# Dense products of a two-block transformer layer: float32 operands once instead of three float32r products of split operands

## The chip, the cores and the metric

The kernel runs on one core of one Trainium2 chip. The metric is device time in microseconds (us) for one execution of the whole program; the time before is the median of three runs. TensorE (PE) does the matrix products, VectorE (DVE), ScalarE (ACT) and GpSimd (POOL) the elementwise work, SyncE (SP) issues most of the transfers.

## The reference

512 tokens of width 1024 pass through two blocks. All arrays are float32.

```python
# first block
u = rms_norm(x, mix_norm_g) @ w_in                    # 1024 -> 2816
c = conformer_conv(u[..., :512])                      # 31 taps over 256 channels
a = dilated_attention(q, k, v, positions)             # 12 heads of 64, over 512 keys
x = x + concat(rms_norm(c), rms_norm(a)) @ w_out
x = x + memory_cross_attention(rms_norm(x), rms_norm(mem), w_xq, w_xk, w_xv, w_xo)   # 256 memory rows, 4 heads of 256
x = x + hierarchical_moe(rms_norm(x), ...)            # 32 experts, 1024 -> 512 -> 1024, 2 per token
x = rms_norm(x, final_norm_g)
# second block
u = rms_norm(x, norm_mix_g_2) @ w_in_2
ya = forgetting_attention(q, k, v, f)                 # 8 heads of 64, causal
ys = s5(u_ssm, ...)                                   # state space layer, then a gate with w_glu_2
x = x + (gate_a * (ya @ w_proj_attn_2) + gate_s * (ys @ w_proj_ssm_2)) @ w_out_2
x = x + hier_moe(rms_norm(x), ...)                    # 32 experts, 1024 -> 256 -> 1024, 2 per token
```

## The kernel before

The program is one long instruction stream; an order of instructions is worked out when it is built, and tc.issue_after fixes single places by hand. It has four stages, one after the other: dense1 (the first block up to its experts), the first expert layer (Moe, method experts), dense2 (the second block up to its experts), the second expert layer.

Dense products. An operand is kept as two float32r tiles, a rounded part (hi) and the rest (lo). Activations lie transposed in a pair of tiles of 128 x 8 x 512, made by K.pair. K.put (L195) fills one 512-column piece of a pair from PSUM: ScalarE writes hi (L199, L202), VectorE then writes lo, the difference (L200, L203). Weights come in units of 1024 x 256, 1 MB, by K.load_unit (L135, issued by SP at L141) into a ring of two slots, k.wt. K.split (L118) makes hi on ScalarE (L125) and lo on VectorE or, every third time, on GpSimd (L128), in two halves for a unit, in a pool of two buffers. Each product is then three matmuls by K.mm3 (L114, L115, L116): hi with hi, hi with lo, lo with hi.

Two helpers loop over the pieces. K.tok_mm (L172) has the activations stationary and 256 weight columns moving: 8 row chunks x 4 token blocks = 32 products for a unit. K.col_mm (L184) has 128 weight columns stationary and up to 512 tokens moving: 8 chunks x 2 = 16 products for a unit. Counted by the code, there are 1024 products with 256 moving columns: 288 in the nine units of q, k and v of dense1, 128 in memory keys and values, 128 in w_out, 32 in the scores of the memory attention, 128 in w_xo, 64 in v of dense2, 128 in its q and k, 128 in w_out_2 (and these sum to 1024). There are 360 with 512 columns: 32 in the convolution's two units, 64 in w_xq, 16 in the memory attention's values, 32 in the two u units of dense2, 64 in its first gate, 8 in the forget logits (L1836, 8 stationary columns), 16 in w_glu_2, 32 in w_proj_ssm_2, 64 in its second gate, 32 in w_proj_attn_2.

Attention. K.heads_T (L151) splits q and k of two heads, transposes them with 12 float32r transposes (L168) and copies them out with 6 copies on ScalarE (L170); it is called 20 times. The scores of a block of 128 queries are two matmuls, q with k hi and q with k lo (L536, L537 in dense1, 48 blocks of 512 keys; L1974, L1975 in dense2, 32 blocks of 128, 256, 384 and 512 keys). The softmaxed block is transposed by four float32 transposes (L545) and multiplied with v in plain float32 (L552): four products of 64 columns for a block.

Experts. Their products take plain float32 operands already. Two experts share the array, 64 stationary columns each: 8 chunks x 512 columns up (L1086), then down (L1108). The second layer works on one further unit, extra_up, in which one expert has all 128 stationary columns: 8 such products. Weights stream in through slots; the first 18 loads of the first layer and 17 of the second are issued during the dense stage before it. The last expert pairs' outputs go back by a one-hot product in float32r, hi and lo (scatter, L1123, L1124), added to X by VectorE (L1126).

The start of dense2 (L1754 to L1836): X is transposed (L1766) and put into the pair hT; the first unit of w_in_2 is loaded after the last ScalarE step of the expert layer before it (tc.issue_after(k.last.ins), L1824) and split; norms() gives Rb (L1790), by which VectorE scales the unit's results; then come the forget logits and the second u unit.

Of the kernel before, what the change touches and what calls it, by code (L numbers as in the profile page):

```python
# [10 lines left out]
F32 = mybir.dt.float32  # L11
F32R = mybir.dt.float32r
# [3 lines left out]
AF = mybir.ActivationFunctionType  # L16
# [11 lines left out]


def f(ap):  # L30
    return ap.bitcast(F32)
# [27 lines left out]
class K:  # L59
# [9 lines left out]
    def setup(self):  # L69
# [9 lines left out]
        self.identr = c.tile([128, 128], F32R, name="identr")  # L79
        nc.vector.tensor_copy(self.identr, self.ident)  # L80
# [16 lines left out]
    def pair(self, pool):  # L97
        return tuple(pool.tile([128, KC, S], F32R, name="b") for _ in range(2))

# [10 lines left out]
    def mm3(self, out, st, mv, start, stop):  # L110
        nc = self.nc
        sh, sl = st
        mh, ml = mv
        nc.tensor.matmul(out, sh, mh, start=start, stop=False, skip_group_check=True)  # L114
        nc.tensor.matmul(out, sh, ml, start=False, stop=False, skip_group_check=True)  # L115
        nc.tensor.matmul(out, sl, mh, start=False, stop=stop, skip_group_check=True)  # L116

    def split(self, pool, pieces, eng=None):  # L118

        nc = self.nc  # L120
        out = []
        for src, kc, n in pieces:
            hi = pool.tile([128, 4, 256], F32R, name="wh")
            lo = pool.tile([128, 4, 256], F32R, name="wl")
            nc.scalar.activation(hi[:, :kc, :n], src, AF.Copy)  # L125
            self.n += 1
            e = eng or (nc.gpsimd if self.n % 3 == self.pool_mod else nc.vector)
            e.tensor_sub(lo[:, :kc, :n], src, f(hi[:, :kc, :n]))  # L128
            for c in range(kc):
                out.append((hi[:, c, :n], lo[:, c, :n]))  # L130
        return out

    pool_mod = 0

    def load_unit(self, cols, kc=8):  # L135

        t = self.wt().rearrange("p (c n) -> p c n", c=8)
        o = 0
        for c in cols:
            w = c.shape[1]  # L140
            self.nc.sync.dma_start(t[:, :kc, o:o + w], c.rearrange("(c p) n -> p c n", p=128))  # L141
            o += w
        return t[:, :kc, :o]

    def split_unit(self, spool, t, eng=None):
        return self.split(spool, [(t[:, j:j + 4], 4, t.shape[2]) for j in range(0, t.shape[1], 4)], eng)

    def unit(self, spool, cols, kc=8):
        return self.split_unit(spool, self.load_unit(cols, kc))

    def heads_T(self, wk, tpt, r4, qT, kh, kl, i):  # L151


        nc = self.nc
        V = nc.vector
        Rq = wk.tile([128, 2, 2, 2, 64], F32R, name="Rq", bufs=1)
        Rk = wk.tile([128, 2, 2, 2, 2, 64], F32R, name="Rk", bufs=1)
        nc.scalar.activation(Rq[:, :, :, 0], r4[:, :, 0:2], AF.Copy)
        V.tensor_sub(Rq[:, :, :, 1], r4[:, :, 0:2], f(Rq[:, :, :, 0]))
        for t in range(2):  # L160
            nc.scalar.activation(Rk[:, :, :, 0, t], r4[:, :, 2:4], AF.Copy)
            V.tensor_sub(Rk[:, :, :, 1, t], r4[:, :, 2:4], f(Rk[:, :, :, 0, t]))
        for dst, mk in ((qT, lambda b, h: Rq[:, b, h]), (kh, lambda b, h: Rk[:, b, h, 0]), (kl, lambda b, h: Rk[:, b, h, 1])):
            p = tpt()
            for h in range(2):
                for b in range(2):
                    o = (2 * h + b) * 128
                    nc.tensor.transpose(p[:, o:o + 128].bitcast(F32R), mk(b, h).rearrange("p t i -> p (t i)"), self.identr)  # L168
            for h in range(2):
                nc.scalar.activation(dst[h][:, 256 * i:256 * i + 256], p[:, 256 * h:256 * h + 256], AF.Copy)  # L170

    def tok_mm(self, act, ws, tiles, nb, n, first=True, last=True, kcs=None):  # L172
# [3 lines left out]
        for i, c in enumerate(ks):  # L176
            for b in range(nb):
# [43 lines left out]
    def raw_T(self, psum, xb, gcol, hi, lo, nb, tag="tp", tpb=2):  # L221

        nc = self.nc
        for c in range(KC):
# [4 lines left out]
            self.put((hi, lo), np.s_[:, c, :w], ps[:, :w], gcol[:, c:c + 1])  # L229
# [9 lines left out]
    def norm_T(self, work, psum, xb, gcol, hi, lo, nb, tpb=2):  # L239
# [11 lines left out]
        for c in range(KC):  # L251
# [4 lines left out]
            nc.scalar.activation(hi[:, c, :w], ps[:, :w], AF.Copy, scale=gcol[:, c:c + 1])  # L256
            nc.vector.scalar_tensor_tensor(lo[:, c, :w], ps[:, :w], gcol[:, c:c + 1], f(hi[:, c, :w]),
# [1899 lines left out]
```

## Time and profile before

| | us |
|---|---|
| median of the runs (1734.44, 1736.08, 1739.26) | 1736.08 |
| the profiled execution | 1743.17 |
| its span, first to last instruction | 1741.5 |
| PE, busy in the span | 1575.2 |
| VectorE, busy | 769.0 |
| ScalarE, busy | 542.6 |
| GpSimd, busy | 381.8 |

The profiled execution is 7.1 us longer than the median of the runs, and 1.7 us of it lie outside the span. PE's matmuls are pipelined: the listed time of one is longer than the distance from its start to the next one's, so busy time tells that PE had work, not how fast it went through it. The distance of starts in the timeline is the cost of one in a row of them. One line of the source can make more than one matmul record.

### The profile page before, as it was taken

To read this page: it belongs to the slowest core of one execution; us is meant where nothing else is said; L and a number is where in the kernel's file an instruction comes from. 1 tells how busy PE (TensorE), PEld (TensorE's weight loads), DVE (VectorE), ACT (ScalarE), POOL (GpSimd) and SP (SyncE) were. 2 spreads that over 40 slices of the span, in tenths; PEclk is the share of its full clock that TensorE was granted. 3 is DMA by queue.
4 is the path that set the end of the run, shared out by engine and by line. 5 is a ranking of instruction groups with operands and counts; after the bars stand their busy time and mean duration, and the time that the engine had idled before them with its cause. 6 is when DMAs were issued, how large, how long until landed. Compare 5 with 4: busy or idle time off the path is not lost. (4 is left out here: it accounts for less than half of the span.)

```text
span 1741.5 us, 24303 instructions
## 1 busy us (share of the span) xinstructions
PE 1575.2 (90%) x9241; PEld 1073.1 (62%) x9241; DVE 769.0 (44%) x1977; ACT 542.6 (31%) x1207; POOL 381.8 (22%) x525
## 2 busy tenths in 40 slices
PE   7999999999999898888988768999999999898986
PEld 5999999987973333332323346888888894333332
DVE  8985546646374311111101356734664547211224
ACT  5355566535212111010100033242655422111111
POOL 2311111110132641532420031111231411111110
PEclk9999999999989999999999888999999999998997
DMA  6234344124669999999999796527440946999984
GB/s 197 80 112 143 97 133 158 62 97 152 224 193 400 425 425 424 424 424 425 425 424 426 327 152 74 114 74 90 64 71 30 364 158 225 387 417 416 398 342 157
DMA packets 171225, 423.71 MB, mean 243 GB/s; under 512 B 20605, under 2 KB 107828, under 8 KB 143328
## 3 DMA queue, kind: packets, MB, share of 16 engines
q1 hardware_dynamic: 133616, 378.08, 60.0%
q0 software_dynamic: 12080, 24.03, 4.6%
q10 hardware_dynamic: 25408, 20.00, 3.7%
q8 instruction: 74, 1.21, 0.3%
q14 instruction: 47, 0.39, 0.1%
HBM read 403.38 MB, written 35.27 MB: 252 GB/s over the span
## 5 line engine op out<-in xcount | busy, mean ns | idle before, releaser
L1086 PE MATMUL h<-w,xgr 128*64 128x512 f32 (+1 forms) x752 | 220.9, 612 | 22.1 <-DMA w<-in_w_dram 19.7
L1086 PE MATMUL h<-b,xgr 128*64 128x512 f32 x800 | 224.3, 607 | 16.8 <-DMA b<-in_w_dram 15.4
L115 PE MATMUL mm<-wl,b 128*128 128x256 f32 x832 | 236.1, 285 | 3.7 <-POOL wl L128 3.6
L114 PE MATMUL mm<-wh,b 128*128 128x256 f32 x832 | 235.7, 286 | 1.4 <-ACT b L202 0.8
L116 PE MATMUL mm<-wh,b 128*128 128x256 f32 x832 | 234.5, 284 | 0.0
L128 POOL TENSOR_TENSOR wl<-w,wh 128x1024 fp32r<-128x1024 f32 x38 | 99.1, 2610 | 557.2 <-ACT wh L125 487.8
L125 ACT ACTIVATE wh<-w 128x1024 fp32r<-128x1024 f32 x112 | 118.3, 1058 | 171.2 <-PE mm L115 72.0
L115 PEld LDWEIGHTS mm<-wl,b 128*128 128x128 f32 x832 | 158.8, 191 | 5.2 <-POOL wl L128 4.0
L114 PEld LDWEIGHTS mm<-wh,b 128*128 128x128 f32 x832 | 158.2, 191 | 3.4 <-ACT b L202 1.0
L116 PEld LDWEIGHTS mm<-wh,b 128*128 128x128 f32 x832 | 158.3, 191 | 0.6
L1108 PE MATMUL o<-b,hgT 128*64 128x512 f32 x448 | 135.6, 652 | 18.0 <-DVEq L1335 9.3
L1086 PEld LDWEIGHTS h<-b,xgr 128*64 128x64 f32 x800 | 68.8, 138 | 124.9 <-issue 87.9
L1086 PEld LDWEIGHTS h<-w,xgr 128*64 128x64 f32 (+1 forms) x752 | 64.9, 141 | 130.7 <-issue 89.6
L114 PE MATMUL mm<-b,wh 128*128 128x512 f32 x320 | 127.0, 409 | 13.3 <-ACT b L202 11.5
L115 PE MATMUL mm<-b,wh 128*128 128x512 f32 x320 | 129.7, 406 | 1.2 <-DVE b L203 1.2
L116 PE MATMUL mm<-b,wl 128*128 128x512 f32 x320 | 127.2, 401 | 3.0 <-POOL wl L128 2.7
L1090 DVE SCALAR_TENSOR_TENSOR hg<-h,gate,hg 128x512 f32<-128x512 f32 (+1 forms) x32 | 19.7, 617 | 246.9 <-PE h L1086 179.6
L128 DVE TENSOR_TENSOR wl<-w,wh 128x1024 fp32r<-128x1024 f32 x74 | 95.0, 1283 | 53.0 <-ACT wh L125 52.3
L1108 PE MATMUL o<-w,hgT 128*64 128x512 f32 (+1 forms) x328 | 97.7, 629 | 4.4 <-ACT og L1137 2.2
L1108 PEld LDWEIGHTS o<-b,hgT 128*64 128x64 f32 x448 | 41.7, 149 | 85.0 <-issue 72.1
L1089 ACT ACTIVATE hg<-h,gate 128x512 f32<-128x512 f32 (+1 forms) x32 | 18.6, 581 | 215.0 <-PE h L1086 185.3
L114 PEld LDWEIGHTS mm<-b,wh 128*128 128x128 f32 x320 | 61.3, 193 | 28.9 <-ACT b L202 12.2
(673 smaller groups left out, 2769.7 us busy)
## 6 DMA issues: line engine op xcount, KB each, us to landing
b<-in_w_dram SPq DMA_DIRECT2D x106, 1024.0 KB
w<-in_w_dram SPq DMA_DIRECT2D x86, 1024.0 KB
b<-in_w_expert_down_dram SPq DMA_DIRECT2D x20, 1024.0 KB
w<-in_w_expert_gate_dram SPq DMA_DIRECT2D x36, 512.0 KB
w<-in_w_expert_up_dram SPq DMA_DIRECT2D x36, 512.0 KB
w<-in_w_in_dram SPq DMA_DIRECT2D x17, 1024.0 KB
b<-in_w_expert_gate_dram SPq DMA_DIRECT2D x30, 512.0 KB
b<-in_w_expert_up_dram SPq DMA_DIRECT2D x30, 512.0 KB
```

Source lines behind the costliest of these rows:

```text
L114: nc.tensor.matmul(out, sh, mh, start=start, stop=False, skip_group_check=True)
L115: nc.tensor.matmul(out, sh, ml, start=False, stop=False, skip_group_check=True)
L116: nc.tensor.matmul(out, sl, mh, start=False, stop=stop, skip_group_check=True)
L125: nc.scalar.activation(hi[:, :kc, :n], src, AF.Copy)
L128: e.tensor_sub(lo[:, :kc, :n], src, f(hi[:, :kc, :n]))
L1086: nc.tensor.matmul(h[po], xg[:, c, ss], fw[e][c], start=c == 0, stop=c == KC - 1, skip_group_check=True)
L1089: nc.scalar.activation(hg, a, AF.Silu, scale=r)
L1090: nc.vector.scalar_tensor_tensor(hg, b, r, hg, op0=OP.mult, op1=OP.mult)
L1108: nc.tensor.matmul(o[po], hT[:, j, po], W[2][e][half * nt + j], start=j == 0, stop=j == nt - 1, skip_group_check=True)
```

## The change

Every dense product takes its float32 operands as they are, in one matmul call. mm3, the splits of weights and activations, pair and the lo tiles go; put is one instruction, on ScalarE and VectorE in turn; weights lie raw in a ring of four slots. heads_T makes four float32 transposes and two copies, the scores are one call with 64 rows in the contraction. The one-hot products of scatter are one float32 call. The second gate of dense2 (sga) moves from bigR to bigL, and the outputs of its two branches share one tile.

```diff
-    def pair(self, pool):
-        return tuple(pool.tile([128, KC, S], F32R, name="b") for _ in range(2))
+    def big(self, pool):
+        return pool.tile([128, KC, S], F32, name="b")
...
-    def mm3(self, out, st, mv, start, stop):
-        nc = self.nc
-        sh, sl = st
-        mh, ml = mv
-        nc.tensor.matmul(out, sh, mh, start=start, stop=False, skip_group_check=True)
-        nc.tensor.matmul(out, sh, ml, start=False, stop=False, skip_group_check=True)
-        nc.tensor.matmul(out, sl, mh, start=False, stop=stop, skip_group_check=True)
-
-    def split(self, pool, pieces, eng=None):
...
-            nc.scalar.activation(hi[:, :kc, :n], src, AF.Copy)
...
-            e.tensor_sub(lo[:, :kc, :n], src, f(hi[:, :kc, :n]))
...
+    def mm(self, out, st, mv, start, stop):
+        self.nc.tensor.matmul(out, st, mv, start=start, stop=stop, skip_group_check=True)
...
-        for dst, mk in ((qT, lambda b, h: Rq[:, b, h]), (kh, lambda b, h: Rk[:, b, h, 0]), (kl, lambda b, h: Rk[:, b, h, 1])):
-            p = tpt()
-            for h in range(2):
-                for b in range(2):
-                    o = (2 * h + b) * 128
-                    nc.tensor.transpose(p[:, o:o + 128].bitcast(F32R), mk(b, h).rearrange("p t i -> p (t i)"), self.identr)
-            for h in range(2):
-                nc.scalar.activation(dst[h][:, 256 * i:256 * i + 256], p[:, 256 * h:256 * h + 256], AF.Copy)
+        p = tpt()
+        for j in range(2):
+            for b in range(2):
+                o = (2 * j + b) * 128
+                nc.tensor.transpose(p[:, o:o + 128], r4[:, b, 2 * j:2 * j + 2].rearrange("p h i -> p (h i)"), self.ident)
+        nc.scalar.activation(qT[:, 256 * i:256 * i + 256], p[:, 0:256], AF.Copy)
+        nc.vector.tensor_copy(kT[:, 256 * i:256 * i + 256], p[:, 256:512])
...
-                self.mm3(o, (act[0][:, c, bs], act[1][:, c, bs]), (ws[i][0][:, :n], ws[i][1][:, :n]), st, sp)
+                self.mm(o, act[:, c, bs], ws[i][:, :n], st, sp)
...
-                self.mm3(o, (ws[c][0][:, ms], ws[c][1][:, ms]), (act[0][:, act_c0 + c, :width], act[1][:, act_c0 + c, :width]), st, sp)
-
-    def put(self, dst, dsl, ps, scale=None):
+                self.mm(o, ws[c][:, ms], act[:, act_c0 + c, :width], st, sp)
+
+    def put(self, dst, ps, scale=None):
+
         nc = self.nc
-        h, l = dst[0][dsl], dst[1][dsl]
+        self.n += 1
+        if self.n % 2:
+            return nc.scalar.activation(dst, ps, AF.Copy, scale=1.0 if scale is None else scale)
         if scale is None:
-            nc.scalar.activation(h, ps, AF.Copy)
-            return nc.vector.tensor_sub(l, ps, f(h))
-        else:
-            nc.scalar.activation(h, ps, AF.Copy, scale=scale)
-            return nc.vector.scalar_tensor_tensor(l, ps, scale, f(h), op0=OP.mult, op1=OP.subtract)
+            return nc.vector.tensor_copy(dst, ps)
+        return nc.vector.tensor_scalar(dst, ps, scale, None, op0=OP.mult)
...
-        spool = k.pool("splA", 2, st, side="right")
+        k.wt = Slots([k.ring] * 2 + [k.pool("ringA", 2, st, side="right")] * 2)
...
-                    nc.tensor.matmul(p, qT[:, bs], kh, start=True, stop=False)
-                    marks.append(nc.tensor.matmul(p, qT[:, bs], kl, start=False, stop=True).ins)
+                    marks.append(nc.tensor.matmul(p, qT[:, bs], kT, start=True, stop=True).ins)
...
-            oh, ol = og[:, 0], og[:, 1]
-            self.k.last = nc.scalar.activation(oh, outs[half], AF.Copy, scale=gate)
-            nc.vector.scalar_tensor_tensor(ol, outs[half], gate, f(oh), op0=OP.mult, op1=OP.subtract)
+            self.k.last = nc.scalar.activation(og[:, half], outs[half], AF.Copy, scale=gate)
...
-                nc.tensor.matmul(y, sT[:, bs], oh, start=True, stop=False)
-                nc.tensor.matmul(y, sT[:, bs], ol, start=False, stop=True)
+                nc.tensor.matmul(y, sT[:, bs], og[:, half], start=True, stop=True)
...
-        spool = k.pool("splD", 2, st)
+        k.wt = Slots([k.ring] * 2 + [k.pool("ringD", 2, st)] * 2)
...
         with tc.issue_after(k.last.ins):
-            ws = k.split_unit(spool, k.load_unit([w_in[:, 1544:1800]]), G)
+            ws = k.load_unit([w_in[:, 1544:1800]])
...
-        ysT = k.big_r.tile([128, KC, S], F32R, name="b")
-        ysT = (ysT[:, 0:4], ysT[:, 4:8])
+        yT = k.big(k.big_r)
+        ysT, yaT = yT[:, 0:4], yT[:, 4:8]
...
-        sga = k.big_r.tile([128, KC, S], F32, name="b")
-        yaT = k.big_r.tile([128, KC, S], F32R, name="b")
-        yaT = (yaT[:, 0:4], yaT[:, 4:8])
+        sga = k.big(k.big_l)
```

## Rows read from the trace of the kernel before

**Rows 1.** The page: busy share of PE and of the transfers in 40 slices, in tenths.
```profile
PE   7999999999999898888988768999999999898986
...
DMA  6234344124669999999999796527440946999984
```

**Rows 2.** Busy time by stage: dense1, experts, dense2, experts; experts' middle; dense2's start.
```profile
core 0: us, PE busy (x) PEld busy (x) DVE busy (x) ACT busy (x) POOL busy (x), PEclk, DMA share, GB/s
0.00:495.00 495.00, 468.86 (x3518) 440.72 (x3518) 303.27 (x661) 247.08 (x562) 90.05 (x97) 0.98 0.41 134
495.00:1011.40 516.40, 450.14 (x1974) 180.37 (x1974) 138.27 (x463) 64.60 (x141) 154.95 (x267) 0.97 0.97 395
1011.40:1432.00 420.60, 392.51 (x2645) 343.92 (x2643) 226.54 (x504) 179.24 (x372) 93.67 (x86) 0.96 0.54 117
1432.00:1741.50 309.50, 263.72 (x1106) 108.09 (x1106) 100.93 (x353) 51.72 (x132) 43.11 (x76) 0.91 0.85 336
522.00:958.00 436.00, 382.69 (x1665) 144.66 (x1663) 89.08 (x300) 54.58 (x121) 146.83 (x254) 0.98 1.01 422
...
1011.40:1066.00 54.60, 36.07 (x143) 25.02 (x142) 38.46 (x129) 15.25 (x30) 17.47 (x18) 0.75 0.84 145
```

**Rows 3.** Groups of PE's instructions by line and form: the split products' largest.
```profile
L115 PE MATMUL mm<-wl,b 128*128 128x256 f32 x832 | 236.1, 285 | 3.7 <-POOL wl L128 3.6 <-DVE wl L128 0.2
L115 PE MATMUL mm<-b,wh 128*128 128x512 f32 x320 | 129.7, 406 | 1.2 <-DVE b L203 1.2
```

**Rows 4.** Timeline of PE, two stretches of float32r products (start us, us): first and last.
```profile
1198.81 0.28 PE L114 MATMUL mm<-wh,b 128*128 128x256 f32 x1
...
1199.89 0.28 PE L114 MATMUL mm<-wh,b 128*128 128x256 f32 x1
...
1175.73 0.40 PE L116 MATMUL mm<-b,wl 128*128 128x512 f32 x1
...
1178.06 0.40 PE L116 MATMUL mm<-b,wl 128*128 128x512 f32 x1
```

**Rows 5.** Float32 products, PE's groups by form: an expert with the whole array; attention's values.
```profile
L1086 PE MATMUL h<-w,xgr 128*128 128x512 f32 x16 | 8.8, 674 | 0.5 <-ACT xgr L1182 0.5
L552 PE MATMUL po<-v,pT 128*128 128x64 f32 x384 | 48.4, 272 | 0.1
```

**Rows 6.** Timeline of PE: float32 records of 512 and 64 columns in a row.
```profile
1627.85 2.74 PE L1086 MATMUL h<-w,xgr 128*128 128x512 f32 x6
...
308.93 1.00 PE L552 MATMUL po<-v,pT 128*128 128x64 f32 x8
```

**Rows 7.** Timeline of PE: transposes in a row, of float32 (L545) and float32r (L168).
```profile
186.03 1.04 PE L545 MATMUL tp<-ident,ml 128*128 128x128 f32 x8
...
1319.15 0.87 PE L168 MATMUL tp<-identr,Rk 128*128 128x128 f32 x8
```

**Rows 8.** PE's waits, whole span: us in total, times, longest.
```profile
PE mm L114 <- ACT b L202: 12.3, 2, 11.5
...
PE y L1123 <- DVE X L1126: 5.0, 6, 1.7
...
PE mm L115 <- POOL wl L128: 3.8, 3, 2.7
...
PE tp L1790 <- DVE r L1787: 3.4, 1, 3.4
PE mm L116 <- POOL wl L128: 2.7, 1, 2.7
...
PE mm L114 <- ACT wh L125: 2.0, 4, 1.0
```

**Rows 9.** Timeline, start of dense2.
```profile
1011.40 1.03 PE L1766 MATMUL tp<-ident,X 128*128 128x128 f32 x8
...
1020.06 2.00 ACT L125 ACTIVATE wh<-w 128x1024 fp32r<-128x1024 f32 x2 [14.41 <-DMA w<-in_w_in_dram]
...
1023.91 1.22 PE L114 MATMUL mm<-b,wh 128*128 128x512 f32 x2 [11.48 <-ACT b L202]
...
1063.67 0.40 PE L116 MATMUL tp<-b,wfl 128*8 128x512 f32 x1
```

More of the change, by code (lines that the diff above doesn't have):

```diff
@@ L142, in load_unit, with heads_T @@
             o += w
[L143 to L151, printed above, removed]
-        nc = self.nc
[L155 to L162, printed above, removed]
-        for dst, mk in ((qT, lambda b, h: Rq[:, b, h]), (kh, lambda b, h: Rk[:, b, h, 0]), (kl, lambda b, h: Rk[:, b, h, 1])):
-            p = tpt()
-            for h in range(2):
-                for b in range(2):
-                    o = (2 * h + b) * 128
-                    nc.tensor.transpose(p[:, o:o + 128].bitcast(F32R), mk(b, h).rearrange("p t i -> p (t i)"), self.identr)
-            for h in range(2):
-                nc.scalar.activation(dst[h][:, 256 * i:256 * i + 256], p[:, 256 * h:256 * h + 256], AF.Copy)
+        return [t[:, c, :o] for c in range(kc)]
+    def heads_T(self, tpt, r4, qT, kT, i):
+        nc = self.nc
+        p = tpt()
[5 more added lines that the diff above has]
+        nc.vector.tensor_copy(kT[:, 256 * i:256 * i + 256], p[:, 256:512])
     def tok_mm(self, act, ws, tiles, nb, n, first=True, last=True, kcs=None):
@@ L228, in raw_T @@
             w = nb * 128
-            self.put((hi, lo), np.s_[:, c, :w], ps[:, :w], gcol[:, c:c + 1])
+            self.put(out[:, c, :w], ps[:, :w], gcol[:, c:c + 1])
     def inv_rms(self, work, xb, nb, out):
@@ L237, in inv_rms, with norm_T @@
         self.rsq(work, out, ss, 1.0 / D, 1e-6)
-    def norm_T(self, work, psum, xb, gcol, hi, lo, nb, tpb=2):
+    def norm_T(self, work, psum, xb, gcol, out, nb, tpb=2):
         nc = self.nc
@@ L385, in dense1 @@
         kvp = k.pool("kvp", 1, st, side="right")
-        mT = [ring1.tile([128, 2048], F32R, name="w").rearrange("p (c s) -> p c s", c=KC) for _ in range(2)]
+        mT = ring1.tile([128, 2048], F32, name="w").rearrange("p (c s) -> p c s", c=KC)
         kmf = ring1.tile([128, 2048], F32, name="w").rearrange("p (c s) -> p c s", c=KC)
@@ L498, in qk_unit @@
             def qk_unit(g):
-                ws = k.unit(spool, [w_in[:, 512 + g * 128:640 + g * 128], w_in[:, 1280 + g * 128:1408 + g * 128]])
+                ws = k.load_unit([w_in[:, 512 + g * 128:640 + g * 128], w_in[:, 1280 + g * 128:1408 + g * 128]])
                 pss = [mmt(), mmt()]
                 k.tok_mm(hT, ws, pss, NB, 256)
-                qk[g] = [[wk.tile([128, S], F32R, name=n, bufs=3) for h in range(2)] for n in ("qT", "kTh", "kTl")]
-                qT, kh, kl = qk[g]
+                qT, kT = qk[g] = [wk.tile([128, S], F32, name=n, bufs=3) for n in ("qT", "kT")]
                 yield
@@ L833, in route @@
         kp = self.kp = keep
-        self.sel_t, self.i512 = self.spot() if self.spot else [kp.tile([128, S], F32R, name=n) for n in ("sel", "i512")]
-        self.i512 = f(self.i512)
+        self.sel_t, self.i512 = self.spot() if self.spot else [kp.tile([128, S], F32, name=n) for n in ("sel", "i512")]
         nc.gpsimd.iota(self.i512, pattern=[[1, S]], base=1, channel_multiplier=0, allow_small_or_imprecise_dtypes=True)
@@ L1766, in dense2 @@
                 nc.tensor.transpose(p[:, b * 128:(b + 1) * 128], X[:, b, c * 128:(c + 1) * 128], k.ident)
-            puts.append(k.put(hT, np.s_[:, c], p, gm[:, c:c + 1]))
+            puts.append(k.put(hT[:, c], p, gm[:, c:c + 1]))
+        fsq = None
         def norms():
@@ L1794, in col_unit @@
         def col_unit(cols, ws=None):
[L1795 removed]
+            ws = ws or k.load_unit([cols])
             pss = [mmt(), mmt()]
@@ L1830, in dense2 @@
             ssm.WT = ssm.fetch(k.big_r, 0)
-        with tc.issue_after(wfc.ins):
+        with tc.issue_after(fsq.ins):
             ssm.load_M(k.big_r)
@@ L1899, in wide @@
             nc.sync.dma_start(t, w.rearrange("(c p) n -> p c n", p=128))
-            return [k.split(spool, [(t[:, :, o:o + 256], 4, 256)]) for o in (0, 256)]
+            return [[t[:, c, o:o + 256] for c in range(4)] for o in (0, 256)]
         for j, ws in enumerate(wide(a["w_glu_2"][0])):
             pss = [mmt(), mmt()]
-            k.col_mm((yh, yl), ws, pss, 2, S)
+            k.col_mm(yf, ws, pss, 2, S)
             for m in range(2):
@@ L2121, in spot @@
         def spot():
-            t = late.tile([128, 2 * S], F32R, name="ssrow")
+            t = late.tile([128, 2 * S], F32, name="ssrow")
             return t[:, 0:S], t[:, S:]
```

147 lines of the change are left out of this document (54 added, 93 removed).

## The prediction

> **What bounds the kernel now.** First the slices of the page [rows 1]: PE is busy everywhere, while the transfers are near their full share only in two long stretches (slices 13 to 23 and 35 to 38). The table by stage [rows 2] says what the stretches are. In both expert stages the transfers set the pace: in the first one's middle their share is 1.01 and they move 422 GB/s, and the weights of those stages are the same after the change. In dense1 and dense2 the transfers' share is 0.41 and 0.54, PE is busy 468.86 of 495 us and 392.51 of 420.6, and VectorE and ScalarE stand at 54 to 61% and 43 to 50%. So the change is decided in 915.6 us of dense work, on PE. What it gives or takes there shifts the expert stages whole: before each of them the loads that may run ahead are a fixed number, and the transfers idle in the dense stages already.
>
> Busy time can't tell how fast PE is: a float32r record of 256 columns is listed with 285 ns [rows 3], but in a row of them one starts every 1.08/9 = 0.12 us, and one of 512 columns every 2.33/10 = 0.233 us [rows 4]. A product of three records thus costs 0.36 us at 256 columns and 0.70 at 512.
>
> **What a float32 product costs.** The trace has the same kind of call already, with all 128 stationary columns and 512 moving ones: in extra_up. Two things are to be seen there. In a row, six records take 2.74 us with 0.59 for the last, the shortest of that line, so one starts every (2.74 - 0.59)/5 = 0.43 us [rows 6]. And the code makes 8 such products, but the trace has 16 records [rows 5]; likewise attention's values, 4 x 48 = 192 products in the code, have 384, while float32r lines have one record for a call. A plain float32 product is two records. At 512 columns it costs 0.86 us, not 0.43; at 256 columns I take half, 0.43, since the records' time goes with the columns (each record is two passes of about 0.215). A reader who takes the 0.43 of the row for the whole product gets the sign of the whole change wrong.
>
> The Trainium skill, "FP8 and Floating Point Precision", section "TensorE Precision Notes", says that true FP32 takes four passes through the array. The trace agrees: two records of two passes, 0.86 us. If each pass cost a whole float32r record (0.233 and 0.12), a product would cost 0.93 and 0.48 us, and the sum below would be +226 us instead of +145.
>
> **The sum, on PE.** 1024 products of 256 columns (832 of their records on one line in the largest group, the rest in six smaller ones [rows 3]): 0.43 - 0.36 = +0.07 us each, +72. 360 products of 512 columns: 0.86 - 0.70 = +0.16 each, +58. Scores of dense1: 48 calls of 512 columns were two records, 0.47; now 0.86; +19. The contraction of 64 rows takes no column away. Scores of dense2: a head has 128 + 256 + 384 + 512 = 1280 columns, 2.5 times 512; 2.5 x (0.86 - 0.47) x 8 heads = +8. heads_T: 240 float32r transposes at (0.87 - 0.25)/7 = 0.089 us become 80 of float32 at (1.04 - 0.28)/7 = 0.109 [rows 7]; -13. Scatter: one product, 0.86, for two records, 0.47, but its last step is paced by VectorE's adds [rows 8]; +1 for both stages' ends. In all 72 + 58 + 19 + 8 - 13 + 1 = +145 us.
>
> **What comes back.** The splits and the second instruction of put leave ScalarE, VectorE and GpSimd; those engines are hidden behind PE in most places, so only PE's waits for them count. The largest is at the start of dense2 [rows 9]. The eight chunks of hT need ScalarE, whose queue stands behind a split that waits for the first weights until 1020.06; PE idles from 1012.4 to 1023.9, then runs chunk by chunk behind put, waits for GpSimd's lo (2.7 us) and for the norm's chain (3.4) [rows 8], and has done 24 products at 1063.9. Afterwards hT is ready before the weights are, but the weights land no earlier: they are still loaded after the last step of the experts. From 1020.1, 24 x 0.86 = 20.6 us, about 1 of transposes and 3 x 0.86 = 2.5 more if the first three run at 1.2 GHz after PE's wait (an estimate: the granted clock of this stretch is 0.75 now, a mean of that level and 2.4 GHz [rows 2]) give 1044. That is 20 us earlier with products that are 24 x 0.16 = 4 us dearer: 24 us of waiting gone. It takes in the 3.4 us for the norm's chain, which stood behind lo's and splits on VectorE and ScalarE; if that chain is late by 1044, it is what PE waits for next, and holds the second u unit's banks. Elsewhere the named waits on splits and puts [rows 3, 8] are 3.8 + 2.0 + 1.2 + (12.3 - 11.5) = 7.8, less 1 that lies in dense2's start: 7. Short waits that a listed 0.28 us hides in a 0.12 us distance don't show at all; busy time leaves 26 + 28 = 54 us visibly idle in the two stages [rows 2], of which the ones named here are 12.3 + 3.8 + 3.4 + 2.7 + 2.0 + 1.2 = 25. I take 11 for unnamed ones, about a third of what is left. In all 42 come back, with bounds of 20 (the 7, and half of the 24) and 65 (all idle time seen, and 11 unseen).
>
> What else the edit touches costs nothing as I see it. Four raw slots for two: weights come further ahead, at 1 MB per unit and 13.8 us of PE for it (32 x 0.43), 76 GB/s against 422 in the experts' middle [rows 2]. SP waits for a slot with nothing queued behind it but later loads. sga in bigL and one tile for both branches only free space. VectorE takes half the puts and kT's copy, ScalarE the other half; both lose more than they get. If PE were no longer the cover there, the softmax chain of a block would show, but PE gets longer, not shorter.
>
> So 145 - 42 = +103. On the profiled execution's own time that is 1743.2 + 103 = 1846; its time is 7 above the median of the runs, so on the median 1736 + 103 = 1839, say **1840 us**.
>
> **Bounds.** Downwards 145 - 65 = +80: 1816. Upwards: a float32r record of 512 columns costs 0.018 us more than a pass of 0.215, one of 256 columns 0.0125; if each float32 record in the dense stages carried that too, it would be 2 x (0.018 x 408 + 0.0125 x 1024) = +40. With that and only 20 back, 145 + 40 - 20 = +165: 1901.
>
> **Rivals.**
>
> *A float32 product is one record's worth.* Then 512 columns cost 0.43 and 256 cost 0.215: 360 x -0.27 = -97, 1024 x -0.145 = -148, scores -2, heads_T -13, together -260, with some 20 of the waits gone 1736 - 280 = 1456 us. For it: 0.43 is what a row of records shows. Against it: twice the records for every plain float32 product in the trace, in three different lines, and single ones for transposes and float32r. It decides once the dense products have one record each. 5%.
>
> *The waits were the bound, not PE.* If the split engines paced PE so finely that what comes back reaches 145, the time stays at 1736. The place is the unit loop, where PE needs hi and lo of each half unit in turn. Against it: in rows of records nothing stands between them, the fullest of the three engines, VectorE, is busy 61% [rows 2], and 54 us of idle time is all there is to see. It decides from 90 us of unseen waits on. 3%.
>
> *Weight loads come into the open.* Each product loads float32 weights twice. A record of 64 columns in attention starts every (1.00 - 0.27)/7 = 0.104 us [rows 5, 6], where its columns alone would be 0.054; the missing 0.05 is a load that 64 columns don't hide. If it were not hidden behind 256 or 512 columns either, 2 x 0.05 x 1432 = 143 us more: 1983. Against it: at 512 columns with 128 weights the distance is 0.43, nothing over two passes. 3%. The Trainium skill, "TensorE: Matmul & The Clock Gate", section "The mechanism", says that a weight load overlaps a running matmul only when it goes to another row group, which would put these loads in the open; the 0.43 speaks against that.
>
> *The order turns worse.* The program's order is worked out anew with other durations, and PE's queue is strict. Between a block's scores and its transposes lies work of VectorE and ScalarE, which PE covers with a unit's products. If that cover stands in the wrong places, and each of the 80 blocks waits 0.8 us, the mean of PE's waits for VectorE in scatter (5.0/6 [rows 8]), it is 64 us: 1904. Against it: PE is busy 468.86 of 495 us in the stage that holds 48 of these blocks [rows 2], and the products that cover their waits get longer. 5%.
>
> **How the numbers follow.** The forecast has 84%, and its own range is 1816 to 1901. 16% lie outside, half of them near its upper edge, so 8 times in 10 needs hardly more than the range itself: 1808 to 1902. What 0.3% of 1736 (5 us) decides: faster 6% (the one-record case and a little of the second rival), within it 2%, slower 92%.
>
> **What the profile after would show.** 2048 records of 256 columns and 720 of 512 on the new mm line, starting 0.215 and 0.43 us apart; dense1 some 65 us longer (0.07 x 704 + 0.16 x 112 + 19 - 8 = +78, less some 12 that come back), dense2 some 35 longer (0.07 x 320 + 0.16 x 248 + 8 - 5 = +65, less 30); both expert stages as long as before, with the same 420 GB/s in the middle; ScalarE and VectorE under 45% in the dense stages; PE's first product of dense2 within 1 us of the landing of its weights. One record for a product, distances of 0.25 or more at 256 columns, or an expert stage longer by over 10 us would prove the working wrong.

## The result and the profile after

The kernel after takes 1880.64 us (median of 4 runs, 1879.56 to 1883.01), the kernel before in the same comparison 1737.67. The ratio is 1.0824 (95% interval 1.0798 to 1.085): 143 us slower. The forecast was 1840, or +103. The direction and the prices on PE held; of what was to come back most did not, and the size was 40 us short. The profiled execution took 1883.01 us, its span is 1881.3.

First the page's slices of after, PE and the transfers, as in [rows 1].

```profile
PE   8999999999999999888888849999999999988996
DMA  7233334042528999999999872424411542999993
```

PE is as full as before, except for one slice: the 24th (1082 to 1129 us), where dense2 starts, stands at 4 tenths. The tables by stage show what that costs. Its edges are the first product of an expert and the first transpose of X in dense2, which can be found in both traces; the first table is before at these edges, the second after.

```profile
core 0: us, PE busy (x) PEld busy (x) DVE busy (x) ACT busy (x) POOL busy (x), PEclk, DMA share, GB/s
0.00:509.50 509.50, 481.99 (x3612) 453.15 (x3612) 317.19 (x734) 249.98 (x571) 92.86 (x101) 0.97 0.43 137
509.50:1011.40 501.90, 437.01 (x1883) 167.93 (x1882) 124.35 (x390) 61.69 (x132) 152.14 (x263) 0.98 0.97 400
1011.40:1446.30 434.90, 404.53 (x2737) 354.80 (x2735) 239.32 (x573) 183.43 (x382) 93.67 (x86) 0.95 0.54 121
1446.30:1741.50 295.20, 251.71 (x1015) 97.22 (x1014) 88.15 (x283) 47.53 (x122) 43.11 (x76) 0.91 0.86 342
```

```profile
0.00:580.40 580.40, 566.42 (x2699) 432.08 (x2699) 217.90 (x631) 145.82 (x377) 36.87 (x80) 0.99 0.39 120
580.40:1079.85 499.45, 444.17 (x1882) 167.15 (x1882) 120.12 (x386) 61.75 (x132) 153.31 (x263) 0.99 0.99 406
1079.85:1591.80 511.95, 477.74 (x2121) 311.64 (x2119) 174.13 (x512) 102.76 (x251) 42.00 (x65) 0.95 0.37 98
1591.80:1881.30 289.50, 250.21 (x999) 93.12 (x998) 84.02 (x273) 46.90 (x120) 41.61 (x76) 0.95 0.88 348
```

Dense1 is 71 us longer (forecast: some 65), dense2 77 (forecast: some 35), the two expert stages are 2 and 6 us shorter (forecast: as long as before). ScalarE and VectorE fall to 25 and 38% in dense1 and 20 and 34% in dense2, as said. So the miss lies in dense2.

The products themselves are where the prediction put them. PE's groups by form, and two long rows of the timeline:

```profile
L104 PE MATMUL mm<-w,b 128*128 128x256 f32 x1664 | 374.7, 381 | 0.0
L104 PE MATMUL mm<-b,w 128*128 128x512 f32 x640 | 290.8, 607 | 24.3 <-DMA w<-in_w_in_dram 23.6 <-DVE b L157 0.8
L104 PE MATMUL mm<-w 128*128 128x256 f32 x256 | 59.7, 384 | 0.0
L104 PE MATMUL sc<-w,b 128*128 128x256 f32 x128 | 30.3, 382 | 0.8 <-ACT P L661 0.6
L486 PE MATMUL sc<-kT,qT 64*128 64x512 f32 x96 | 49.6, 624 | 0.0
```

```profile
1274.66 24.20 PE L104 MATMUL mm<-b,w 128*128 128x512 f32 x56
...
1298.70 13.54 PE L104 MATMUL mm<-w,b 128*128 128x256 f32 x62
```

1664 + 256 + 128 = 2048 records of 256 columns for 1024 products, and 96 records for 48 score calls: two records for each float32 product. One starts every (24.20 - 0.59)/55 = 0.429 us at 512 columns and every (13.54 - 0.38)/61 = 0.216 at 256; 0.43 and 0.215 were forecast. The second row of the groups holds the miss: 24 us of idle time, nearly all of it for weights in transfer.

Where that is, the timeline of PE at the start of dense2 shows (start, duration, in brackets the idle time before and what ended it):

```profile
1082.90 0.66 PE L1700 MATMUL tp<-ident,X 128*128 128x128 f32 x4 [1.45 <-ACT b L155]
1095.91 3.56 PE L104 MATMUL mm<-b,w 128*128 128x512 f32 x4 [12.36 <-DMA w<-in_w_in_dram]
...
1099.75 1.88 PE L104 MATMUL mm<-b,w 128*128 128x512 f32 x4
...
1117.14 6.61 PE L104 MATMUL mm<-b,w 128*128 128x512 f32 x8 [11.20 <-DMA w<-in_w_in_dram]
```

The chunk of hT that the first product needs is put by 1082.9, long before 1095.91; the weights are not there, as forecast, but they come far later than forecast:

```profile
1082.16 0.69 ACT L155 ACTIVATE b<-tp,gm 128x512 f32<-128x512 f32 x1 [0.72 <-PE tp L1700]
```

PE waits 12.4 us for the first unit's weights and 11.2 for the second's. After the first wait four records take 3.56 us where the next four take 1.88: the granted clock is 0.53 from 1095.9 to 1099.3, the lower of the two levels, and 1.00 from 1099.7 to 1101.5. That costs 1.7 us more.

Why are the weights late? The first unit's load is issued 8.3 us before the stage (1071.5), hardly other than before the change (7.3 us, 1004.1). What moved is another transfer: the table M (load_M, 2 MB, by the code in pieces of 512 bytes), which GpSimd issues. GpSimd's timeline, before and then after:

```profile
1021.20 4.68 POOL L128 TENSOR_TENSOR wl<-w,wh 128x1024 fp32r<-128x1024 f32 x2 [63.74 <-ACT wh L125]
...
1027.87 5.08 POOL L1721 DMA_DIRECT2D b<-scr  x8
```

```profile
1080.16 1.89 POOL L1709 TENSOR_TENSOR st<-ssrow 128x1024 f32<-128x1024 f32 x1 [49.29 <-PE y L1062]
1082.01 5.08 POOL L1659 DMA_DIRECT2D b<-scr  x8
```

Before, GpSimd's queue stood behind its half of the first split, which waits for the landing of the first weights (1020.06 in [rows 9]): M was issued 16.5 us into the stage, after that landing. Without the split nothing holds it, and it is issued 2.2 us into the stage, while the weights are on their way. The queues between 1087 and 1096 (packets, MB, share of the 16 engines):

```profile
q0 software_dynamic: 190, 0.63, 55.0%
q10 hardware_dynamic: 204, 0.42, 32.1%
q1 hardware_dynamic: 205, 0.21, 18.7%
```

M's queue (q0) takes 55%, that of the table WT (q10) 32%, and the weights' queue (q1) moves 0.21 MB in 9 us. Each of the three moved about 200 packets; the mean packet of M has 3.3 KB, that of WT 2.1 and that of the weights 1.0. WT was issued 1.2 us after the first weights before and 1.1 after; M is what moved. That M is the cause was a theory at this point; the experiments test it.

### The profile page after: what moved, and what is told of

The parts are those of the page before. It is cut to its first block, busy times and chain, and to the rows that moved or that the text cites. A ratio compares the mean times of both kernels' runs of the same rounds, so it can differ in the third digit from the quotient of the medians.

```text
span 1881.3 us, 20430 instructions
## 1 busy us (share of the span) xinstructions
PE 1738.5 (92%) x7697; PEld 1004.0 (53%) x7697; DVE 596.2 (32%) x1799; ACT 357.2 (19%) x880; POOL 273.8 (15%) x484
## 5 line engine op out<-in xcount | busy, mean ns | idle before, releaser
L104 PE MATMUL mm<-w,b 128*128 128x256 f32 x1664 | 374.7, 381 | 0.0
L104 PEld LDWEIGHTS mm<-w,b 128*128 128x128 f32 x1664 | 310.9, 190 | 55.8 <-issue 16.2
L104 PE MATMUL mm<-b,w 128*128 128x512 f32 x640 | 290.8, 607 | 24.3 <-DMA w<-in_w_in_dram 23.6
L104 PEld LDWEIGHTS mm<-b,w 128*128 128x128 f32 x640 | 121.4, 195 | 168.1 <-issue 141.1
L1049 PE MATMUL o<-b,hgT 128*64 128x512 f32 x448 | 126.3, 633 | 11.2 <-ACT og L1075 4.5
L490 DVE CUSTOM_DVE_ANT_0 ml<-sc,X 128x512 f32<-128x512 f32 x48 | 33.0, 690 | 86.9 <-PE sc L486 71.5
L104 PE MATMUL mm<-w 128*128 128x256 f32 x256 | 59.7, 384 | 0.0
L104 PEld LDWEIGHTS mm<-w 128*128 128x128 f32 x256 | 47.3, 190 | 14.1 <-issue 8.3
L1115 PEld LDWEIGHTS g<-ident,xr 128*128 128x128 f32 x240 | 34.0, 210 | 38.7 <-issue 28.9
L501 PEld LDWEIGHTS po<-v,pT 128*128 128x128 f32 x384 | 48.0, 192 | 4.4 <-ACT pT L499 2.0
L486 PE MATMUL sc<-kT,qT 64*128 64x512 f32 x96 | 49.6, 624 | 0.0
```

The costliest lines, as they stand in the source:

```text
L104: self.nc.tensor.matmul(out, st, mv, start=start, stop=stop, skip_group_check=True)
L486: marks.append(nc.tensor.matmul(p, qT[:, bs], kT, start=True, stop=True).ins)
L490: V.tensor_tensor_reduce(ml, p, lnm[:, lo:lo + 512], -0.125, 3.0e38, op0=OP.add, op1=OP.min, accum_out=nm)
L501: nc.tensor.matmul(po[:, b], pT[:, kb * 128:(kb + 1) * 128], v[:, kb, o:o + 64], start=b == 0 and kb == 0, stop=b == NB - 1 and kb == 3, s ...
L1049: nc.tensor.matmul(o[po], hT[:, j, po], W[2][e][half * nt + j], start=j == 0, stop=j == nt - 1, skip_group_check=True)
L1115: nc.tensor.transpose(p[:, c], xr[:, self.chan(4 * h + c)], self.k.ident)
```

## The experiments

**Holding M back.** After, with a read of the first unit's weights on GpSimd ahead of load_M.

```
+        gate = G.tensor_copy(st1.tile([128, 1], F32, name="gate"), ws[7][:, 0:1])
-        with tc.issue_after(fsq.ins):
+        with tc.issue_after(gate.ins):
             ssm.load_M(k.big_r)
```

> The kernel after, and GpSimd reads one column of dense2's first weights before it issues the eight transfers of the table M (2 MB in 512-byte pieces), as its split of those weights made it wait in the kernel before. Theory A, that M's transfers, now issued 2 us after the stage's start and no longer 16, take the queue from the weights of dense2's first two units: those land some 16 us after their issue as before, PE's two waits of 12.4 and 11.2 us shrink to some 4 and 0 to 4, and the time falls by 12 to 20 us, to 1861 to 1869. Theory B, that the two units' weights which go ahead in the two new slots hold up the first unit's: M's transfers don't matter, 1878 to 1884. Theory C, that the prediction's 24 us never were PE's to get: also no change.

Measured: 1872.77 us (1861.36 to 1888.32), ratio to before 1.0754 (1.0712 to 1.0796). In the profiled run the first product comes 4.8 us after the stage's start instead of 16.1, and the second wait stays (11.4 us). The first half of theory A holds; the gate only passed the collision on to the second unit. The runs differ by 27 us, and the profiled one is the slowest: its dense2 is as long as that of the kernel after (511 us), since what it wins at the stage's start it loses again, most plainly between 1430 and 1480 us, where its granted clock is 0.70, a mean of the two levels (0.93 in the kernel after from 1440 to 1490). Why it falls there is not shown.

**Weights of the first units earlier.** After, with the slots in the other order.

```
-        k.wt = Slots([k.ring] * 2 + [k.pool("ringD", 2, st)] * 2)
+        k.wt = Slots([k.pool("ringD", 2, st)] * 2 + [k.ring] * 2)
...
-        with tc.issue_after(k.last.ins):
-            ws = k.load_unit([w_in[:, 1544:1800]])
+        ws = k.load_unit([w_in[:, 1544:1800]])
```

> The kernel after, with dense2's slots in the other order: the first two units' weights go to the two slots that come free 15 us earlier (issue at 1056.6 and 1057.0 instead of 1071.5 and 1072.4), the third and fourth to the two that the experts' last products hold. If PE's 23.6 us of waits for weights are all that dense2's start lost, both go, with some 3 us at the lower clock behind them: 1853 to 1857. Rival: the wait moves on to the third unit's weights, which now land as late as 1096 to 1117, while PE needs them at 1084 + 2 x 13.8 = 1112: then only 18 to 22 us come back, 1859 to 1863. If PE's waits for weights were a cover for a later chain (norm, M, the SSM's tables): under 10 us, 1871 or more.

Measured: 1856.76 us (1855.08 to 1857.51), 1.0683 (1.0657 to 1.0708), 24 us below the kernel after. PE's row at the same place:

```profile
1084.40 0.66 PE L1700 MATMUL tp<-ident,X 128*128 128x128 f32 x4 [1.45 <-ACT b L155]
1084.89 2.74 PE L104 MATMUL mm<-b,w 128*128 128x512 f32 x6
```

No wait for weights is left, though M is issued 2.2 us into the stage as in the kernel after. The first 24 products of the two u units and the 8 of the forget logits are done 33.9 us after the stage's start at 1081.35; before it was 52.5. That is 19 us earlier with products that are 32 x 0.16 = 5 dearer: 24 us of waiting are gone. The prediction's 24 were worked out otherwise, and wrongly; the part on the prediction comes back to it.

**Two slots instead of four.** After, with `k.wt = Slots([k.ring] * 2)` in dense2.

> The kernel after with two raw slots in dense2, as before, and not four. Theory B, that the two loads which go ahead hold up the first unit's weights: the first product comes 8 us earlier and the time falls by 8 to 15 us, 1866 to 1873. Theory A (M's transfers do it): the first product comes as late as now within 3 us; later units are loaded one slot at a time, 13.8 us of products against 2.6 us at 400 GB/s, so no further loss: 1878 to 1884. If the extra slots are worth something in the rest of dense2: slower than 1885.

Measured: 1881.04 us (1879.12 to 1886.67), 1.0829 (1.0797 to 1.0862). The time is theory A's, but not its place: the first product comes 4.9 us after the stage's start, and the expert stage before is 14 us longer. GpSimd and PE there:

```profile
1064.86 5.08 POOL L1659 DMA_DIRECT2D b<-scr  x8
```

```profile
1072.07 1.93 PE L1049 MATMUL o<-w,hgT 128*64 128x512 f32 x4 [1.83 <-DMA w<-in_w_dram]
1081.57 4.99 PE L1049 MATMUL o<-w,hgT 128*64 128x512 f32 x12 [7.57 <-DMA w<-in_w_dram]
```

Here M is issued 29 us before the stage's start (1094.09), and now, while M is under way, it is the last expert's weights that land late. Since M moved together with the slots, this run can't clear the two loads that go ahead in the additional slots (theory B); the next one can, since it keeps them.

**Holding M behind the second unit.** After, with the gate on that unit's weights.

```
+        w1u = k.load_unit([w_in[:, 1800:2056]])
+        gate = G.tensor_copy(st1.tile([128, 1], F32, name="gate"), w1u[7][:, 0:1])
-        with tc.issue_after(fsq.ins):
+        with tc.issue_after(gate.ins):
             ssm.load_M(k.big_r)
...
-        u_unit(1)
+        u_unit(1, w1u)
```

> The kernel after, and GpSimd reads one column of dense2's second unit's weights (not the first's, as in the first gate) before it issues M's eight transfers. If M's transfers are what both of PE's waits for weights are about, both go, as with the weights loaded early (1857): 1853 to 1862, and less spread between runs than the first gate's 1861 to 1888. Rival: M now collides with the loads of later units, and PE waits for one of those: 1866 or more. Rival: M itself is what is late, the SSM's outputs wait for it: a wait for M of over 5 us in the list, 1866 or more.

Measured: 1862.27 us (1857.87 to 1864.06), 1.0705 (1.0675 to 1.0736). Of the two waits 1.3 us is left, with the weights' own loads issued as in the kernel after (8.3 and 7.5 us before the stage's start) and the two loads in the additional slots ahead of them as there:

```profile
1086.07 1.98 PE L104 MATMUL mm<-b,w 128*128 128x512 f32 x4
...
1095.81 3.70 PE L104 MATMUL mm<-b,w 128*128 128x512 f32 x8 [1.29 <-DMA w<-in_w_in_dram]
```

```profile
1095.82 0.18 POOL L1769 COPY gate<-w 128x1 f32<-128x1 f32 x1 [10.00 <-DMA w<-in_w_in_dram]
1096.67 5.08 POOL L1659 DMA_DIRECT2D b<-scr  x8 [0.67 <-DMA b<-sWT]
```

The second unit's weights have landed by 1095.8, 13.5 us into the stage; in the kernel after they landed 37 us into it. So M's place settles when the weights land, and theory B falls.

**The same collision in the kernel before.** The first split is queued behind hT's puts on ScalarE; without and with a gate ahead of load_M.

```
-            nc.scalar.activation(h, ps, AF.Copy, scale=scale)
+            self.hi = nc.scalar.activation(h, ps, AF.Copy, scale=scale)
...
-        with tc.issue_after(k.last.ins):
-            ws = k.split_unit(spool, k.load_unit([w_in[:, 1544:1800]]), G)
+        ws = k.load_unit([w_in[:, 1544:1800]])
+        with tc.issue_after(k.hi.ins):
+            ws = k.split_unit(spool, ws, G)
```

The gate, against the kernel without it:

```
-            G.tensor_tensor(fq, frow, frow, op=OP.mult)
+            k.fsq = G.tensor_tensor(fq, frow, frow, op=OP.mult)
...
-        ws = k.load_unit([w_in[:, 1544:1800]])
+        ws = wu = k.load_unit([w_in[:, 1544:1800]])
...
-        with tc.issue_after(wfc.ins):
+        with tc.issue_after(k.fsq.ins):
+            gate = G.tensor_copy(st1.tile([128, 1], F32, name="gate"), wu[:, 7, 0:1])
+        with tc.issue_after(gate.ins):
             ssm.load_M(k.big_r)
```

> The kernel before, with the split of dense2's first weights queued on ScalarE behind the eight puts of hT, so that the puts don't wait for the weights' landing. GpSimd's half of the split comes later too, so M's transfers are no longer held behind the weights' landing. The prediction's reading alone (PE waits 11.5 us for ScalarE, then chunk by chunk): 12 to 20 us come back, 1717 to 1726. With the collision that the kernel after showed, now in the old kernel: the weights of the first two units land later by some 8 and 20 us and eat it up: 1734 to 1748.

> The same edit, and GpSimd reads one column of the first weights before it issues M's transfers, which holds them until the landing, as the split did in the kernel before. The puts' 11.5 us come back and nothing collides with the first unit's weights: 8 to 15 us faster than before, 1722 to 1730. If the collision has no part in it, this is the same as the kernel without the gate, within 3 us.

Measured: without the gate 1746.66 us, 1.0048 (1.0028 to 1.0069), 0.5% slower; with it 1734.34, 0.9978 (0.9958 to 0.9998), 0.2% faster, which is hardly clear of noise. ScalarE's splits of the first and the second unit, without the gate and with it, and last that of the second unit in the kernel before:

```profile
1024.92 1.99 ACT L125 ACTIVATE wh<-w 128x1024 fp32r<-128x1024 f32 x2
1049.62 1.06 ACT L125 ACTIVATE wh<-w 128x1024 fp32r<-128x1024 f32 x1 [22.71 <-DMA w<-in_w_in_dram]
```

```profile
1021.83 1.99 ACT L125 ACTIVATE wh<-w 128x1024 fp32r<-128x1024 f32 x2
1037.70 1.06 ACT L125 ACTIVATE wh<-w 128x1024 fp32r<-128x1024 f32 x1 [13.88 <-DMA w<-in_w_in_dram]
```

```profile
1034.20 1.04 ACT L125 ACTIVATE wh<-w 128x1024 fp32r<-128x1024 f32 x1
```

M issued at 1013.6, 1018.8 and 1027.9 (in these two and in the kernel before) goes with second weights that land at 1049.6, 1037.7 and no later than 1034.2, where ScalarE splits them without a wait. The direction is as expected; the gain of 3 us is not 8 to 15: the second unit's weights are still held, as ScalarE's wait of 13.9 us for them shows.

**Holding M behind the second unit in the kernel before.** Against the kernel with the first gate: the gate reads the second unit's weights, and that unit's load is written ahead of it.

```
+        w1u = k.load_unit([w_in[:, 1800:2056]])
         with tc.issue_after(k.fsq.ins):
-            gate = G.tensor_copy(st1.tile([128, 1], F32, name="gate"), wu[:, 7, 0:1])
+            gate = G.tensor_copy(st1.tile([128, 1], F32, name="gate"), w1u[:, 7, 0:1])
...
-        u_unit(1)
+        u_unit(1, k.split_unit(spool, w1u))
```

> The kernel before with the puts of hT ahead of the first split, as in the last two kernels, and M's transfers held until the second unit's weights have landed. With the first unit's gate alone, the second unit's weights landed 28 us into the stage and PE's first 24 products ended at 47 (before: 52). If M's transfers are what holds the second unit's weights, they land by 16 to 18, the 24 products end at 36 to 40, and the time is 8 to 15 us below before: 1722 to 1729. Rival: the transfer of the table WT (2 MB, issued 1 us after the first weights) holds them as well: 1732 to 1738, no gain.

Measured: 1739.14 us, 1.0007 (0.9993 to 1.002): no gain, but not for the rival's reason. The second weights land 17.5 us into the stage, as expected. Then this wait is the longest among PE's products:

```profile
PE mm L116 <- POOL wl L128: 10.0, 1, 10.0
```

The first unit's low part stands on GpSimd behind the gate and the issue of M's eight transfers (5 us), and ends at 1039. In this order GpSimd's queue can't hold M without holding the split behind it; the split ahead of the gate was not tried.

**The price of the products, splits kept.** Before, with one float32 product of parts in each unit.

```
+    def mm1(self, out, st, mv, start, stop, c):
+        self.nc.tensor.matmul(out, f(st[c % 2]), f(mv[1 - c % 2]), start=start, stop=stop, skip_group_check=True)
...
-                self.mm3(o, (act[0][:, c, bs], act[1][:, c, bs]), (ws[i][0][:, :n], ws[i][1][:, :n]), st, sp)
+                self.mm1(o, (act[0][:, c, bs], act[1][:, c, bs]), (ws[i][0][:, :n], ws[i][1][:, :n]), st, sp, c)
```

> The kernel before with all its splits and puts, but each unit's product is one float32 product of two of the parts (alternately hi with lo and lo with hi, so that PE still waits for both; the other parts' products are left out). 992 products of 256 columns and 336 of 512; scores, transposes and scatter as before. The prediction's prices: 992 x 0.07 + 336 x 0.16 = +123 us, 1861; with the distances in the trace after (0.432 for 0.355, 0.858 for 0.697): 992 x 0.077 + 336 x 0.161 = +130, 1868. If PE's waits for the splits shrink because PE is slower even with the splits kept: 1845 to 1855. If the price lies elsewhere (scores, order, waits of the new kernel): under 1830.

Measured: 1887.90 us (1885.98 to 1889.65), 1.0861 (1.0834 to 1.0887): +151, 20 to 27 us over what was expected. The units' records start 0.216 and 0.429 us apart here too. Dense2 is 66 us longer, near the 62 that the distances give; dense1 is 86 longer, where they give 65. There PE's idle time grows from 27.5 to 40.3 us, 13 of the 21 that are over. The longest waits for ScalarE and GpSimd in that stage:

```profile
PE g L1201 <- ACT xgr L1202: 5.2, 1, 5.2
PE po L555 <- ACT pT L553: 4.6, 3, 2.8
...
PE mm L119 <- POOL wl L131: 3.5, 1, 3.5
PE sc L114 <- ACT P L722: 3.1, 2, 2.2
```

Slower products did not cover the splits better. That the order of the program, worked out anew, is what left the new waits is the likely reason; it was not tried.

**Heads and scores alone, and scatter alone.** Before, with the new heads_T and scores; before, with the new scatter. The edits are those of the change's diff.

> The kernel before with the new heads' transposes and scores alone (four float32 transposes for twelve, one float32 product over 64 rows for two of float32r; q and k are no longer split). The prediction's terms: 19 + 8 - 13 = +14 us on PE, 1752; with the distances in the trace after (scores 41.3 and 18.2 us for 22.4 and 9.5, transposes 8.7 for 19.0): +17, 1755. If the fewer instructions of ScalarE and VectorE ahead of each score give PE's waits back: 1740 to 1748. If 64 rows were cheaper than 128: under 1738.

> The kernel before with the new scatter alone: one float32 product for two of float32r, no low part on VectorE. The prediction's price: +1 us, 1737 to 1740. Rival: the expert stages of the kernel after, 8 us shorter together, got it from here (VectorE's low part no longer stands between an expert's last product and the adds): 1729 to 1733.

Measured: heads and scores 1756.99 us, 1.0109 (1.0078 to 1.014), +20 with +14 forecast, inside the interval; 64 rows are no cheaper than 128. A lone call is even dearer than the 0.86 of the sum. In the kernel after:

```profile
92.83 1.12 PE L486 MATMUL sc<-kT,qT 64*128 64x512 f32 x2
93.88 0.66 PE L494 MATMUL tp<-ident,ml 128*128 128x128 f32 x4
```

From its start to that of the next instruction the call takes 1.05 us; the distance is 0.43 only inside a run of several score calls. Four records of 128 rows between transposes in the same trace take 1.72 (1099.75 to 1101.47), 0.43 each. Why the calls of 64 rows lose 0.2 us there is not shown. An estimate from the distances of all score records is 69 us in the kernel after and 39 in the kernel before, +30 where the sum has +27.

Scatter 1735.70 us, 0.9993 (0.998 to 1.0006): nothing, as forecast, and the shorter expert stages don't come from it (503 and 292 us in its profile).

**One record for a product.** Before, with two of the three products left out.

```
-        nc.tensor.matmul(out, sh, mh, start=start, stop=False, skip_group_check=True)
-        nc.tensor.matmul(out, sh, ml, start=False, stop=False, skip_group_check=True)
-        nc.tensor.matmul(out, sl, mh, start=False, stop=stop, skip_group_check=True)
+        nc.tensor.matmul(out, sh, mh, start=start, stop=stop, skip_group_check=True)
```

> The kernel before with all its splits and puts, and only the first of each unit's three float32r products (the other two are left out): a product of one record. If PE alone set the dense stages: 1024 x (0.117 - 0.355) + 360 x (0.233 - 0.697) = -411 us, 1326. The splits keep ScalarE, VectorE and GpSimd as busy as before; VectorE's 303 + 227 us in the two dense stages (916 us) leave at most -386. If the engines of the splits pace PE finely already in the kernel before, as the prediction's second rival has it: hardly faster, over 1650. My own guess lies between: 1400 to 1550.

Measured: 1564.94 us (1554.27 to 1566.23), 0.8993 (0.8969 to 0.9018): 171 us less and not 411, 15 us above the guess. A row of its products, its longest wait and its dense1:

```profile
36.50 3.97 PE L114 MATMUL mm<-wh,b 128*128 128x256 f32 x32
```

```profile
PE mm L114 <- ACT wh L123: 46.6, 16, 11.9
```

```profile
0.00:412.00 412.00, 316.33 (x1978) 275.01 (x1978) 323.78 (x734) 247.26 (x571) 93.05 (x104) 0.84 0.53 170
```

A float32r record costs (3.97 - 0.28)/31 = 0.119 us here, 0.357 for three. With the products down to a third, VectorE is busy 79% of dense1, PE waits for the weights' high part, and its granted clock falls to 0.84: now PE waits for the splits. The same splits stand in the kernel before, whose time lies 171 us above that: they are not what bounds it.

## Why the prediction was right and where not

**Two records for a product, PE the bound.** Right. With the measured distances the terms are 1024 x (0.431 - 0.357) = +76 (72 forecast) and 360 x (0.858 - 0.70) = +57 (58); with scores, transposes and scatter as forecast the sum is 76 + 57 + 27 - 13 + 1 = +148 for +145; the estimate for the scores adds 3. (The smaller groups of 256-column records beside the 832 are four on each line, not six; the count of 1024 stands.) The Trainium skill, "FP8 and Floating Point Precision", section "TensorE Precision Notes", has four passes for true FP32; 0.858 us in two records, 3.7 times a float32r record of 0.233, agrees with it as far as a total can.

**24 us come back at dense2's start.** This is the step that failed, and twice. First its count is wrong. By 1063.9 the kernel before had done 32 products of dense2, not 24; PE's groups from 1011.4 to 1064:

```profile
L115 PE MATMUL mm<-b,wh 128*128 128x512 f32 x24 | 11.5, 477 | 0.0
...
L115 PE MATMUL tp<-b,wfh 128*8 128x512 f32 x8 | 3.9, 482 | 0.0
```

These are 24 products of the two u units and 8 of the forget logits. The prediction's own working gives 1020.1 + 32 x 0.86 + 1 + 2.5 = 1051 for them: 13 us earlier, with products 5 dearer, 18 us of waiting gone and not 24, and +109 in all. Second, and more, the prediction took the landing of the weights as fixed ("the weights land no earlier") and asked only who waits for them. It did not ask what the removed split had held back on GpSimd, the engine that issues M. M's transfers moved 14 us forward in the stage and ran into the weights: what was gained at ScalarE was lost at the landing (12.4 + 11.2 us, and the slower clock behind them). Three experiments bear it out from different sides: earlier weights (1857), M held back (1862), and M let loose in the kernel before (1747 for 1737). That 24 us of waiting do go with the earlier weights is luck: there the first product comes 3.5 us into the stage, where the prediction let the weights land 8.7 us into it.

**The range.** Of the 42 us that were to come back, 148 - 143 = 5 did, fewer than the lower bound of 20. The result lies inside the range only because its upper end also held 40 us for dearer records, and the distances show none. That the range held is luck too.

**"SP waits for a slot with nothing queued behind it but later loads."** Nothing here speaks against it for SP; what the four slots gain or cost by themselves is not shown, since M moved too when there were two (1881). What the section on the kernel says of the first unit, that it is loaded after the experts' last step because of the issue order, was a misreading. In the kernel before the load goes out at 1004.06, ahead of ScalarE's last step there; what SP's queue waited for is the experts' last products, which hold the slot:

```profile
SPq L141 <- PE o L1108: 23.7, 2, 23.3
```

```profile
1004.96 0.69 ACT L1118 ACTIVATE og<-o,gate 128x512 fp32r<-128x512 f32 x1 [2.74 <-PE o L1108]
```

With a slot that comes free earlier (and without the issue order) it went 15 us earlier.

**The unnamed waits.** By the measured distances dense1 should be 704 x 0.074 + 112 x 0.158 + 19 - 8 = 81 us longer, and it is 71: 10 came back, 12 were forecast for that stage. Dense2 should be 66 longer and is 77. With the weights early it is 482.7 us, 48 longer, so 18 of 30 came back there: 24 at the stage's start, and the rest of the stage is some 6 over its price, the cause of which stays open. In all that version stands at +119, 16 over the forecast of +103: 3 from the sum (6 with the scores' estimate), the rest from waits that did not come back. How many waits there are is not a property of the kernel before: with splits kept and slower products it is some 24 more (the price experiment), so what the removal of the splits is worth can't be read from one trace.

**The rivals.** One record for a product: no, two are in the trace. (The run with one record for a product does not test its 1456: its records are float32r, and the splits stayed in that kernel.) The waits as the bound: no, by that same run. Weight loads in the open: no, the distances leave nothing for them. The order turning worse: not in the kernel after, where PE is idle for 14 us of dense1, but the price experiment makes it likely that it can.

**Expert stages.** "As long as before" was forecast, and they are 8 us shorter together. The second one lasts 285 to 295 us in the profiles of the six variants of the kernel before that leave it alone, so this is not shown to be the change's.

## What to carry to other kernels

Count the records that a call makes before you price it: a plain float32 product is two records here, and three float32r products at 0.27 of its price each are cheaper. When an edit takes a wait off an engine, list everything that was queued behind it on that engine, transfers above all: a wait can be what keeps a low-priority transfer out of the way of one that PE needs next. If it was, put the gate back on purpose, or get the needed transfer out early.

## What the runs showed of the hardware

- The 2 MB of M on GpSimd's queue held 55% of the transfer engines at 70 GB/s (0.63 MB in 9 us), and the weights' queue moved 23 GB/s beside them. Alone, behind the second unit's gate (1097 to 1110 us), they held 96.5% at 108 GB/s, where the experts' weights move 422.
- A float32 record takes 0.216 us at 256 columns and 0.429 at 512, with new 128-column weights for each: nothing is lost at the smaller size, while float32r goes from 0.233 to 0.119 and loses 2%.
- A float32 score product over 64 rows is no cheaper than one over 128 rows: 0.43 us a record inside a run of its kind, and 1.05 us for the two records of a lone call (92.83 to 93.88).
